# Attention with a bias on one core: the order of the first-pass loads and the place of the last two V copies

## The chip, the core and the metric

The kernel runs on one core of a Trainium2 chip. The metric is the device time of one execution in microseconds. A core has five engines that each work through a program of their own, in order: PE (TensorE, matmuls; its weight loads are listed as PEld), ACT (ScalarE, here the exps), DVE (VectorE), POOL (GpSimd, here only loads) and SP (SyncE, here copies inside the core's memory and stores). They wait for each other by semaphores. Sixteen DMA engines move the data that the queues of POOL, SP and ACT hand them.

## The reference

```python
head_dim = q.shape[-1]                      # q, k, v: (4, 8, 1024, 64), bias: (1, 1, 1024, 1024), float32
scale = 1.0 / np.sqrt(head_dim)
scores = scale * np.matmul(q, k.transpose(0, 1, 3, 2))
scores = scores + bias
scores_max = np.max(scores, axis=-1, keepdims=True)
attn = np.exp(scores - scores_max) / (np.sum(np.exp(scores - scores_max), axis=-1, keepdims=True) + 1e-8)
return np.matmul(attn, v).astype(np.float32)
```

There are 32 heads, and all of them share one bias of 1024 by 1024.

## The kernel before

**Slots.** The 32 heads are 16 pairs, and the 1024 queries of a head are 8 chunks of 128. One chunk of one head is a slot: a tile of 1024 keys by 128 queries of transposed scores. There are 256 slots. PSUM holds three such tiles, the places 0, 1 and 2 (`places`), and slots go to them in turn.

**The bias stays in the place.** A place works through the heads with one chunk. The bias of the chunk is put in once, by eight matmuls with the identity, at a start slot; for the next head PE adds the new head's K times Q and takes the old head's away, in one set of eight matmuls whose 128 contraction rows are 64 of the new head (`ko`, `qo`) and 64 of the old one with its sign turned (`ke`, `qe`). So a fill is 8 matmuls, at a start slot 16. A slot's fill has to wait until the slot before it in the same place has been read.

**Passes.** The first seven pairs go through chunks 0, 1 and 2 (slots 0 to 41), then 3 and 4 (slots 42 to 69, with start slots 42, 43 and 44, which need bias chunks 3 and 4), then 5, 6 and 7 (start slots 70, 71 and 72). The other nine pairs follow from slot 112 on: pair 14 begins at slot 154, pair 15 at slot 160.

**Exp and AV.** ACT reads a place and writes the exp as bf16 (`E`, a ring of 13). For 20 of the 256 slots DVE does it in six steps instead (`d_steps`: `dy`, `df`, `dt`, `df`, `dt`, `de`); only the first, `dy`, reads the place, so it is the one that lets the next fill in. These are called D slots; slots 38, 47, 50 and 150 are among them. Then PE multiplies the exp with V (AV, 8 matmuls into `po`). `vall` has a column of ones beside each head's V, which gives the sum. DVE divides (`rs`, `ob`; an evacuation of up to seven slots) and SP stores.

**Operands.** K and Q arrive as float32, are cast to bf16 by the loading DMA, are transposed by PE (`px`) and copied out by DVE (`ko`, `qo`) and, for the old head's half, by DVE or by an SP copy (`ke`, `qe`). Q of pairs 0 and 1 is loaded in two parts: the first three chunks at the beginning, the other five later as the rest (`qrest0`, `qrest1`), which is needed from slot 42 on. V is loaded into a ring of two tiles (`vland`) and copied by DVE into `vall` (line 492), so V of a pair is loaded no earlier than the copy of V of the pair two before.

**Loads.** All loads after the first few go through POOL's queue, in order. Those of the first pass are issued one after the other (`early`), as the list near the end of the kernel has them; each stands only for its buffer and its semaphore. From K of pair 7 on, `issue` puts a one-element copy to `tick` ahead of a load (line 467): it reads the load that lies two back in `flight`, so POOL issues nothing more until that has landed, and two loads at most are in flight.

**The order of the instructions** is made when the program is built. A planner walks through time with prices written by hand for each step and with estimated landing times of the loads (`raw_at` for K and Q, `vland_at` for V, `bias_at`). At each point it gives PE, ACT, DVE or SP the next step that is due by this reckoning. What it reckons sets the order only: on the chip each engine takes its steps in that order and waits where one is not ready. DVE's steps lie in `dve_q` with the time from which each may run and a priority; `move_v` enters the copy of V with the estimated landing. Which slots of place 2 become D slots is decided in `pe_cands`, in the kernel before by `backlog`, DVE's outstanding work.

Of the kernel before, what the change touches and what calls it, by code (L numbers as in the profile page):

```python
# [16 lines left out]
def kernel(  # L17
# [13 lines left out]
    nc = tc.nc  # L31
    B, H, S, D = q.shape
    P = 128
    NCH = S // P
# [13 lines left out]
    SPLIT, EARLY = 2, 7  # L48
# [3 lines left out]
    C0 = 3  # L52
# [17 lines left out]
    tick = consts.tile([1, 1], BF)  # L70
# [18 lines left out]
    slots = []  # L89
# [20 lines left out]
    NS = len(slots)  # L110
# [10 lines left out]
        at_place[x[0]] = s  # L121

    dslots = set()
    may_d = [x[0] == 2 and 36 < s < NS - 18 and not any(y[3] for y in slots[s:s + 4]) for s, x in enumerate(slots)]

    raws, lands, arrs = {}, {}, {}

# [18 lines left out]
    def load_q(pr, cs):  # L148
        if pr >= EARLY and 0 in BESIDE:
            return beside(pr, 0)  # L150

        t = consts.tile([P, 2, NCH - C0, D], BF, name=f"qrest{pr}") if cs.start else land.tile([P, 2, NCH, D], BF, name="q16")
        lands[pr, 0, cs.start] = t
        to = t[:, :, :cs.stop - cs.start, :]
        nc.gpsimd.dma_start(out=to.rearrange("p t c d -> p t (c d)"),
                            in_=qf[pr][:, :, cs.start * D:cs.stop * D])
        return to[:1, 1, cs.stop - cs.start - 1, D - 1:]
# [177 lines left out]
    with tc.manual_schedule():  # L335
# [101 lines left out]
        sp_q, t_sp = [], T0  # L437
        AHEAD, SLACK = 60, 300
        DEP = 115
        ROOM = 5000  # L440
        MARGIN = 0
        WINDOW = 4

# [17 lines left out]

        def issue(at, cost, depth, load, pr, *a):

            nonlocal t_dma
            if 0 < depth <= len(flight):
                what, t = flight[-depth]
                nc.gpsimd.tensor_copy(tick[:], what)  # L467
                at = max(at, t + 100)
            at = pool(at, 750)
            t_dma = max(t_dma + cost, at + 2200 + cost)  # L470
            flight.append((load(pr, *a), t_dma + 200))
            return t_dma + 200
# [17 lines left out]
        def move_v(pr):  # L490
            def run(t2):
                nc.vector.tensor_copy(vall[:, 2 * pr % VR:2 * pr % VR + 2, :, :D], lands[pr, "v"][:])  # L492
                v_at[pr] = t2 + 480 + L_DVE
                next_v(v_at[pr])
            dve_q.append((vland_at[pr], 0.3, 480, run))


        def early(kind, pr):
            if kind == "k":
                raw_at[pr, 1, 0] = issue(0, 1600, 0, load_k, pr) + SLACK  # L500
            elif kind == "q":
                cs = slice(0 if pr >= SPLIT else C0, NCH)
                raw_at[pr, 0, cs.start] = issue(0, 1600 if pr >= SPLIT else 1100, 0, load_q, pr, cs) + SLACK
            elif kind == "v":
                vland_at[pr] = issue(0, 1600, 0, load_v, pr)
                move_v(pr)
            else:
                bias_at[pr] = issue(0, 1600, 0, load_b, pr)

        def doubles(pr, which, c0, n, t2, urgent):  # L510
            if not which and pr >= EARLY:
# [63 lines left out]
        def pe_cands():  # L575

            out = []
            for x in range(3):
                if not queue[x] or queue[x][0] > next_fill + WINDOW:
                    continue  # L580
                s = queue[x][0]
                r = fill_ready(s)
                if r is not None and (before[s] is None or before[s] in used):
                    cost = FILL + BIAS * bool(slots[s][3] and s > 1)

                    def do(t, s=s, x=x, cost=cost):
                        nonlocal next_fill
                        fill(s)
                        filled[s] = t + cost + L_PE
                        queue[x].pop(0)  # L590
                        next_fill = min([y[0] for y in queue.values() if y], default=NS)
                        if may_d[s] and backlog(t) < ROOM and len(open_d) < 3:
                            dslots.add(s)
                            avq.remove(s)
                            start_d(s)
                        else:
                            acts.append(s)
                    out.append((max(t_pe, r), cost, do, 0, s))
# [92 lines left out]

        chains, d_wait, open_d = [], [], set()

        def backlog(t):
            x = max(0, t_dve - t) + sum(y[2] for y in dve_q if y[0] < t + 3000 and y[1] < 3)
            return x + sum(sum(y[0] for y in c) for c in chains) / 2 + sum(sum(y[0] for y in c[1:]) for r, s, c in d_wait) / 2

        def start_d(s):
            steps = d_steps(s)
            open_d.add(s)  # L700
# [68 lines left out]
        move_v(0)  # L769
        for x in ("k3", "q3", "v1", "k4", "q4", "v2", "k5", "q5", "v3", "k6", "q6", "v4", "v5", "b3", "q0", "q1", "b4", "v6", "b5", "b6", "b7"):  # L770
            early(x[0], int(x[1]))
        while next_fill < NS or next_act < len(acts) or avq or dav or dve_q or sp_q:
            c = []
            if next_act < len(acts):

                s = min(x for x in acts[next_act:] if filled[x] <= max(t_act, filled[acts[next_act]]))
                acts.remove(s)
                acts.insert(next_act, s)
                if next_act < NE or acts[next_act - NE] in av_done:
                    r = max(t_act, filled[s], av_done[acts[next_act - NE]] if next_act >= NE else 0)  # L780
# [62 lines left out]
```

## Time and profile before

| | |
|---|---|
| time, median of 3 runs (lowest to highest) | 233.25 us (232.87 to 233.69) |
| the profiled execution: its own time, its span | 235.16 us, 233.4 us |
| PE busy | 222.3 us (95%) |
| ACT busy | 221.1 us (95%), 237 exps of it 218.0 |
| DVE busy | 201.5 us (86%) |
| POOL busy | 63.4 us (27%) |
| DMA, HBM read and written | 29.36 MB and 8.39 MB |
| granted clock of PE | 0.997 |

The profile is of one execution and its times count from the beginning of the span. In a timeline each row has the start, the length, the engine, the line of the kernel, the operation with the tiles it writes and reads, the number of instructions put together in the row, and in brackets how long the engine had been idle just before and what ended that. "Busy" of a DMA in POOL's queue is the issue alone; its landing is given apart. The time of a run and the span of the profiled execution are not the same thing: a difference in the span is carried over to the median.

### The profile page before, as it was taken

How to read it: one execution, taken by the hardware profiler on the slowest of the kernel's cores; microseconds unless marked ns; L12 is line 12 of the kernel's file. 1: busy time of each engine (PE TensorE's matmuls, PEld its weight loads, DVE VectorE, ACT ScalarE, POOL GpSimd, SP SyncE). 2: the span in 40 equal slices, each digit the busy share in tenths (PEclk: the TensorE clock that was granted, in tenths of full speed). 3: DMA queues.
4: the chain of work that ended last, by engine and by line, in shares of the span. 5: the costliest groups of instructions: out<-in, count | busy, mean ns of one | idle time of the engine just before them, and what ended most of it. 6: DMA issues, size and time to landing. Idle time of an engine off the chain costs nothing. (4 is left out here: it accounts for less than half of the span.)

```text
span 233.4 us, 10703 instructions
## 1 busy us (share of the span) xinstructions
PE 222.3 (95%) x4671; PEld 209.3 (90%) x4671; DVE 201.5 (86%) x296; ACT 221.1 (95%) x241; POOL 63.4 (27%) x99
## 2 busy tenths in 40 slices
PE   7989999899999999999999997999999999999992
PEld 2869999798999999999999997999999999999982
DVE  2576677599999998999999869999998999999972
ACT  3799999988999999999999998999999999999993
POOL 8943135055446555245352310000000000000000
PEclk9999999999999999999999999999999999999998
DMA  6999979959999899999999992111111111221212
GB/s 206 206 205 215 224 166 158 229 121 150 120 191 137 131 159 183 204 196 157 197 163 201 204 194 68 44 42 39 44 37 42 45 42 42 65 59 42 66 48 56
DMA packets 55646, 29.75 MB, mean 127 GB/s; under 512 B 31472, under 2 KB 51952, under 8 KB 55600
## 3 DMA queue, kind: packets, MB, share of 16 engines
q0 software_dynamic: 30336, 14.06, 48.7%
q1 hardware_dynamic: 24832, 14.40, 22.6%
q8 instruction: 36, 0.59, 1.1%
q10 hardware_dynamic: 432, 0.62, 0.8%
q14 instruction: 10, 0.08, 0.1%
HBM read 29.36 MB, written 8.39 MB: 162 GB/s over the span
## 5 line engine op out<-in xcount | busy, mean ns | idle before, releaser
L258 ACT ACTIVATE E<-pl 128x1024 bf16<-128x1024 f32 (+1 forms) x237 | 218.0, 1089 | 4.3 <-PE pl L244 3.9
L312 PE MATMUL po<-vall,E 128*128 128x65 bf16 x1888 | 93.6, 194 | 0.9 <-ACT E L258 0.9
L312 PEld LDWEIGHTS <-E 128*128 128x128 bf16 x1888 | 78.1, 98 | 1.9 <-ACT E L258 1.2
L244 PE MATMUL pl<-qo,ko 128*128 128x128 bf16 x1024 | 77.3, 219 | 1.7 <-DVE dy L275 1.1
L244 PEld LDWEIGHTS <-ko 128*128 128x128 bf16 x1160 | 69.2, 98 | 4.5 <-issue 1.5
L244 PE MATMUL pl<-qe,ke 128*128 128x128 bf16 x888 | 66.8, 219 | 1.9 <-DVE qe L212 0.5
L244 PEld LDWEIGHTS <-ke 128*128 128x128 bf16 x888 | 53.2, 98 | 5.0 <-issue 1.3
L275 DVE TENSOR_SCALAR dy<-pl 128x1024 int32<-128x1024 f32 x20 | 24.4, 1220 | 2.1 <-PE pl L244 1.4
L322 DVE TENSOR_TENSOR ob<-po,rs 128x448 f32<-128x448 f32 (+2 forms) x39 | 23.2, 594 | 1.9 <-DVE rs L320 0.5
L295 DVE SCALAR_TENSOR_TENSOR de<-dy,dt 128x1024 uint16<-128x1024 int32 x20 | 24.4, 1218 | 0.0
L290 DVE SCALAR_TENSOR_TENSOR dt<-df,dt 128x1024 f32<-128x1024 f32 x20 | 24.4, 1218 | 0.0
L284 DVE SCALAR_TENSOR_TENSOR dt<-df 128x1024 f32<-128x1024 f32 x20 | 24.3, 1217 | 0.0
L287 DVE SCALAR_TENSOR_TENSOR df<-dt,df 128x1024 f32<-128x1024 f32 x20 | 24.3, 1216 | 0.0
L199 DVE COPY ko<-px 128x1024 bf16<-128x1024 bf16 (+1 forms) x16 | 10.7, 671 | 6.9 <-PE px L191 6.3
L165 POOL DMA_DIRECT2D v<-in_v_dram x16 | 11.4, 712 | 18.3 <-DVE vall L492 16.0
L138 POOL DMA_DIRECT2D q<-in_q_dram x18 | 16.0, 890 | 1.3 <-DMA out_dram<-ob 0.5
L201 DVE TENSOR_SCALAR qo<-px,sgn 128x1024 bf16<-128x1024 bf16 (+2 forms) x18 | 12.4, 688 | 4.4 <-PE px L191 3.6
L280 DVE TENSOR_SCALAR df<-dy 128x1024 f32<-128x1024 uint16 x20 | 13.8, 690 | 0.0
L241 PE MATMUL pl<-ident,braw 128*128 128x128 bf16 x136 | 11.5, 228 | 0.1
L145 POOL DMA_DIRECT2D k<-in_k_dram x15 | 11.0, 734 | 2.2 <-PE pl L244 1.0
L320 DVE RECIPROCAL rs<-po 128x7 f32<-128x7 f32 (+3 forms) x40 | 7.8, 195 | 4.4 <-PE po L312 4.0
L467 POOL COPY tick<-q 1x1 bf16<-1x1 bf16 x9 | 3.8, 421 | 24.7 <-DMA q<-in_q_dram 24.7
(54 smaller groups left out, 129.5 us busy)
## 6 DMA issues: line engine op xcount, KB each, us to landing
v<-in_v_dram POOLq DMA_DIRECT2D x16, 256.0 KB, 6.1
k<-in_k_dram POOLq DMA_DIRECT2D x15, 256.0 KB, 5.6
out_dram<-ob SPq DMA_DIRECT2D x32, 96.0 KB, 3.6
out_dram<-ob SPq DMA_DIRECT2D x45, 64.0 KB, 3.2
ke<-ko SPq DMA_DIRECT2D x22, 128.0 KB, 4.9
q<-in_q_dram POOLq DMA_DIRECT2D x18, 128.0 KB, 4.8
qe<-q SPq DMA_DIRECT2D x17, 128.0 KB, 4.9
out_dram<-ob SPq DMA_DIRECT2D x67, 32.0 KB, 1.8
```

Source lines behind the costliest of these rows:

```text
L138: nc.gpsimd.dma_start(out=t[:, :, y, :], in_=(qf, kf)[x][pr][:, y].rearrange("p (c d) -> p c d", d=D))
L201: nc.vector.tensor_scalar(t["qo"][:, cs, :], px[:], sgn[:], None, op0=ALU.mult)
L244: nc.tensor.matmul(to, kk[:, kc, :], qq[:, c, :], start=False, stop=True, skip_group_check=True)
L258: nc.scalar.activation(e[:, i:i + n].rearrange("p b x -> p (b x)"), places[slots[s][0]][:, i:i + n].rearrange("p b x -> p (b x)"), ACTF.Ex ...
L275: w.tensor_scalar(t["y"][:], places[slots[s][0]].rearrange("p b x -> p (b x)"), scale * LOG2E * 65536.0, 127.0 * 65536.0, op0=ALU.mult, op ...
L280: w.tensor_scalar(t["f"][:], t["lo"], G / 65536.0, None, op0=ALU.mult)
L284: w.scalar_tensor_tensor(t["t"][:], t["f"][:], -G, t["f"][:], op0=ALU.add, op1=ALU.mult)
L287: w.scalar_tensor_tensor(t["f"][:], t["t"][:], Q, t["f"][:], op0=ALU.mult, op1=ALU.add)
L290: w.scalar_tensor_tensor(t["t"][:], t["f"][:], V, t["t"][:], op0=ALU.add, op1=ALU.mult)
L295: w.scalar_tensor_tensor(etile[s].bitcast(U16).rearrange("p c q -> p (c q)"), t["y"][:], 1.0 / 512.0, t["t"][:], op0=ALU.mult, op1=ALU.add)
L312: nc.tensor.matmul(po[:, j + i, :], etile[s][:, kc, :], vall[:, slots[s][2] % VR, kc, :], start=j + i + kc == 0, stop=kc == NCH - 1, skip_ ...
L322: nc.vector.tensor_tensor(ob[:, :n, :], po[:, :n, :D], rs[:, :n, :].to_broadcast([P, n, D]), op=ALU.mult)
```

## The change

The early loads are taken out of the planning function `early`, which now only reckons, and are issued in a second loop in another order: the rests of Q of pairs 0 and 1 come ahead of V of pair 5 (before, they came behind V of pair 5 and bias chunk 3). The loads behind them, bias chunks 3 and 4, V of pair 6 and bias chunks 5 to 7, each get a copy to `tick` that reads the load two back, as the later loads have it. The planner's landing times of these loads stay as they were. Its entries in `flight` now carry other times, so that it reckons the loads from K of pair 7 on with landings 1.6 us later. The copies of V of pairs 14 and 15 may be placed 2.5 us later than before. The D slots are a list, `PLAN`, in place of the rule; it holds the same 20 slots that the rule chose.

```diff
@@ -121,9 +121,8 @@
     dslots = set()
-    may_d = [x[0] == 2 and 36 < s < NS - 18 and not any(y[3] for y in slots[s:s + 4]) for s, x in enumerate(slots)]
+    PLAN = (38, 47, 50, 59, 75, 78, 96, 108, 117, 129, 150, 159, 171, 177, 189, 195, 207, 216, 225, 234)
...
@@ -461,14 +459,17 @@
         def issue(at, cost, depth, load, pr, *a):
-            nonlocal t_dma
             if 0 < depth <= len(flight):
                 what, t = flight[-depth]
                 nc.gpsimd.tensor_copy(tick[:], what)
                 at = max(at, t + 100)
-            at = pool(at, 750)
-            t_dma = max(t_dma + cost, at + 2200 + cost)
-            flight.append((load(pr, *a), t_dma + 200))
+            t = lands_at(at, cost)
+            flight.append((load(pr, *a), t))
+            return t
+
+        def lands_at(at, cost):
+            nonlocal t_dma
+            t_dma = max(t_dma + cost, pool(at, 750) + 2200 + cost)
             return t_dma + 200
@@ -492,20 +493,24 @@
-            dve_q.append((vland_at[pr], 0.3, 480, run))
+            dve_q.append((vland_at[pr] + 2500 * (pr >= 14), 0.3, 480, run))
         def early(kind, pr):
             if kind == "k":
-                raw_at[pr, 1, 0] = issue(0, 1600, 0, load_k, pr) + SLACK
+                raw_at[pr, 1, 0] = lands_at(0, 1600) + SLACK
...
+        def early_load(kind, pr):
+            if kind == "q":
+                return load_q(pr, slice(0 if pr >= SPLIT else C0, NCH))
+            return {"k": load_k, "v": load_v, "b": load_b}[kind](pr)
@@ -589,7 +594,7 @@
-                        if may_d[s] and backlog(t) < ROOM and len(open_d) < 3:
+                        if s in PLAN:
@@ -769,6 +770,12 @@
         for x in ("k3", "q3", "v1", "k4", "q4", "v2", "k5", "q5", "v3", "k6", "q6", "v4", "v5", "b3", "q0", "q1", "b4", "v6", "b5", "b6", "b7"):
             early(x[0], int(x[1]))
+
+        for x in ("k3", "q3", "v1", "k4", "q4", "v2", "k5", "q5", "v3", "k6", "q6", "v4", "q0", "q1", "v5"):
+            flight.append((early_load(x[0], int(x[1])), t_dma))
+        for x in ("b3", "b4", "v6", "b5", "b6", "b7"):
+            nc.gpsimd.tensor_copy(tick[:], flight[-2][0])
+            flight.append((early_load(x[0], int(x[1])), t_dma + 200))
```

In the program that this builds, PE, DVE and ACT have the same instructions as before. PE's and DVE's order is the same for the first 82 us of the profile before; from there on K and Q pieces, V copies and D steps of pairs 7 to 15 stand some steps earlier or later. ACT's queue ends with one more store.

More of the change, by code (lines that the diff above doesn't have):

```diff
@@ L439 @@
         DEP = 115
-        ROOM = 5000
         MARGIN = 0
@@ L494, in run @@
                 next_v(v_at[pr])
-            dve_q.append((vland_at[pr], 0.3, 480, run))
+            dve_q.append((vland_at[pr] + 2500 * (pr >= 14), 0.3, 480, run))
         def early(kind, pr):
             if kind == "k":
-                raw_at[pr, 1, 0] = issue(0, 1600, 0, load_k, pr) + SLACK
+                raw_at[pr, 1, 0] = lands_at(0, 1600) + SLACK
             elif kind == "q":
-                cs = slice(0 if pr >= SPLIT else C0, NCH)
-                raw_at[pr, 0, cs.start] = issue(0, 1600 if pr >= SPLIT else 1100, 0, load_q, pr, cs) + SLACK
+                raw_at[pr, 0, 0 if pr >= SPLIT else C0] = lands_at(0, 1600 if pr >= SPLIT else 1100) + SLACK
             elif kind == "v":
-                vland_at[pr] = issue(0, 1600, 0, load_v, pr)
+                vland_at[pr] = lands_at(0, 1600)
                 move_v(pr)
             else:
-                bias_at[pr] = issue(0, 1600, 0, load_b, pr)
+                bias_at[pr] = lands_at(0, 1600)
+        def early_load(kind, pr):
+            if kind == "q":
+                return load_q(pr, slice(0 if pr >= SPLIT else C0, NCH))
+            return {"k": load_k, "v": load_v, "b": load_b}[kind](pr)
         def doubles(pr, which, c0, n, t2, urgent):
@@ L692 @@
         chains, d_wait, open_d = [], [], set()
-        def backlog(t):
-            x = max(0, t_dve - t) + sum(y[2] for y in dve_q if y[0] < t + 3000 and y[1] < 3)
-            return x + sum(sum(y[0] for y in c) for c in chains) / 2 + sum(sum(y[0] for y in c[1:]) for r, s, c in d_wait) / 2
         def start_d(s):
```

## The prediction

> **What bounds the kernel now.** I read the page first: one line of busy time, one row of the DMA engines in 40 slices of 5.8 us.
>
> ```profile
> PE 222.3 (95%) x4671; PEld 209.3 (90%) x4671; DVE 201.5 (86%) x296; ACT 221.1 (95%) x241; POOL 63.4 (27%) x99
> ...
> DMA  6999979959999899999999992111111111221212
> ```
>
> ACT and PE are both at 95%, DVE at 86%. Loads keep the DMA engines at nine tenths up to slice 24, with two dips in the first pass: slice 5 (29.2 to 35.0 us) and slice 8 (46.7 to 52.5). Next, ACT's timeline, to see where the busiest engine stands still (first column start, then length; in brackets the idle time just before).
>
> ```profile
> 17.19 30.08 ACT L258 ACTIVATE E<-pl 128x1024 bf16<-128x1024 f32 x32 [0.21 <-PE pl L244]
> 47.53 1.02 ACT L258 ACTIVATE E<-pl 128x1024 bf16<-128x1024 f32 x1 [0.26 <-PE pl L244]
> 48.76 1.02 ACT L258 ACTIVATE E<-pl 128x1024 bf16<-128x1024 f32 x1 [0.21 <-PE pl L244]
> 50.00 4.69 ACT L258 ACTIVATE E<-pl 128x1024 bf16<-128x1024 f32 x5 [0.21 <-PE pl L244]
> 55.28 17.52 ACT L258 ACTIVATE E<-pl 128x1024 bf16<-128x1024 f32 x19 [0.59 <-PE pl L244]
> ...
> 143.24 86.31 ACT L258 ACTIVATE E<-pl 128x1024 bf16<-128x1024 f32 x94 [0.87 <-PE pl L244]
> ```
>
> Unhindered, exps start 0.904 us apart (start times in the trace). Where ACT stood, the next slots are 42 to 44 (0.26, 0.21, 0.21), slot 51 (0.59) and slot 153 (0.87), always for a fill of PE. So I looked at what held PE and DVE there: PE at 42, DVE up to 53, and PE at 54.
>
> ```profile
> 42.11 0.47 PE L191 MATMUL px<-ident,qrest 128*64 128x128 bf16 x10 [0.78 <-DMA qrest<-in_q_dram]
> ```
>
> ```profile
> 42.62 0.55 DVE L201 TENSOR_SCALAR qo<-px,sgn 128x640 bf16<-128x640 bf16 x1 [1.88 <-PE px L191]
> ...
> 46.96 0.43 DVE L492 COPY vall<-v 128x1024 bf16<-128x1024 bf16 x1 [0.85 <-DMA v<-in_v_dram]
> ...
> 52.86 1.22 DVE L275 TENSOR_SCALAR dy<-pl 128x1024 int32<-128x1024 f32 x1
> ```
>
> ```profile
> 53.35 0.42 PE L312 MATMUL po<-vall,E 128*128 128x65 bf16 x8
> 54.13 0.61 PE L244 MATMUL pl<-qe,ke 128*128 128x128 bf16 x8 [0.36 <-DVE dy L275]
> 54.57 0.61 PE L244 MATMUL pl<-qo,ko 128*128 128x128 bf16 x8
> ```
>
> PE ended its AV at 41.33 and stood 0.78 for the rest of q of pair 0. DVE stood 1.88 behind that, then 0.85 for V of pair 6 (landed 46.9), and from 46.96 worked without a gap until the `dy` of slot 47 was done at 54.08; the fill of slot 50 waited for that one, and slot 51's exp behind it. The third place, DVE and then PE:
>
> ```profile
> 133.61 0.43 DVE L492 COPY vall<-v 128x1024 bf16<-128x1024 bf16 x1 [0.40 <-DMA v<-in_v_dram]
> ...
> 138.33 0.43 DVE L492 COPY vall<-v 128x1024 bf16<-128x1024 bf16 x1 [1.86 <-DMA v<-in_v_dram]
> ...
> 141.32 1.22 DVE L275 TENSOR_SCALAR dy<-pl 128x1024 int32<-128x1024 f32 x1
> ```
>
> ```profile
> 142.59 0.61 PE L244 MATMUL pl<-qo,ko 128*128 128x128 bf16 x8 [1.14 <-DVE dy L275]
> ```
>
> DVE stood 0.40 for V of pair 13 and 1.86 for V of pair 14; `dy` of slot 150 came at 141.32 though its fill had ended at 139.84, PE waited 1.14 for the place, and exp 153 started 1.94 after its predecessor: 1.94 - 0.904 = 1.03 lost. Last, POOL's timeline for the loads of the first pass:
>
> ```profile
> 27.20 0.70 POOL L165 DMA_DIRECT2D v<-in_v_dram  x1 [4.39 <-DVE vall L492]
> 32.77 0.74 POOL L165 DMA_DIRECT2D v<-in_v_dram  x1 [4.88 <-DVE vall L492]
> ...
> 34.05 1.42 POOL L155 DMA_DIRECT2D qrest<-in_q_dram  x2
> ...
> 36.02 0.70 POOL L165 DMA_DIRECT2D v<-in_v_dram  x1
> ```
>
> The V at 32.77 is pair 5's. It stood 4.88 for the copy of V of pair 3, with eight loads queued behind it in order; the DMA engines were at 0.37 from 32 to 34 us.
>
> **The change, part by part.**
>
> *The rests go first.* POOL is free from 27.90. With the rests ahead of V5 they issue at 27.9 and 28.6, not 34.05 and 34.75. V5 is not moved: its wait ends at 32.5 either way. The rests queue behind V4, which landed at 32.9; they had landed 1.3 apart (42.0 and 43.3), so they land at about 34.2 and 35.5 (call the second T). Bounds of T: 34.3, if they slip in beside V4, and 37.8, if the first takes the 3.6 us that lay between bias chunk 3 (38.4) and it. V5 came 4.0 after its issue and was copied at 36.89; behind the rests it lands by about 37, and DVE's idle 0.89 before its next step (38.19) covers that; beyond 0.9 it would cost what it exceeds.
>
> PE's transposes of the rest then start at 41.33. Everything behind moves up 0.78, except where ACT has not freed the place: slot 39's fill (43.67) needs slot 36's exp (42.09, took 1.04, unmoved) to end at 43.13, so from there the gain is 0.54. The bias fills of slots 42 to 44 are 1.23 apart on PE and stay so: exp 44 moves from 50.00 to 49.46.
>
> *Loads from bias chunk 3 on wait for all but the last two.* POOL gets six one-element copies to `tick` (0.18 to 1.09 each, means 0.42 to 0.86 by tile; I take 0.5): 3 us on an engine busy 27%, which by itself costs nothing. What counts is who is queued behind. Chunk 3 waits for the second rest, chunk 4 for V5, V6 for chunk 3, chunks 5 to 7 for chunk 4, V6 and chunk 5. Issue to landing with little in flight was 4.0 (V5), 4.9 (chunk 3), 3.9 (K7); I take 4.4. Chunk 3 lands at T + 0.5 + 4.4 = 40.4, needed at 45.8; chunk 4 at about 42, needed at 47.0; V6 at L = T + 2 x (0.5 + 4.4) = 45.3, not 46.9. Bounds of L: 34.3 + 2 x (0.2 + 3.9) = 42.5, and 37.8 + 2 x (1.1 + 4.9) = 49.8. Chunks 5 to 7 land at about 46.5, 50 and 51 and are used from slot 70 on (exp at 71.6); K7 and Q7 go out near 50 and 51, as before.
>
> If each of the two ticks waited behind a whole long DVE step (1.22), L would be 46.7 and the gain below 0.2 (rival 1). I stay with 0.5, since DVE's steps from 35 to 41 are 0.2 to 0.75 long. The Trainium skill (SBUF — State Buffer, section SBUF: two separate sides) gives the reason for such a wait: VectorE and GpSimd lock each other out of a shared port pair for a whole instruction; the trace's 1.09 against 0.18 for one element fits.
>
> *DVE in the first pass.* With the rest early DVE reaches V6's copy at 46.11 - 0.78 = 45.33. `dy` of slot 47 was the end of the gapless run, so it moves by 46.96 minus the larger of 45.33 and L, but no earlier than its fill, which ends at 52.02 - 0.54 = 51.48: 51.6, not 52.86, if V6 lands by 45.6. Then slot 50's place is free at 52.83 and its fill no longer waits for DVE; it follows AV 36 (53.35 - 0.54 + 0.26 = 53.07), slot 51's fill 0.44 later, its exp 0.71 after that: 54.22, not 55.28. **Gain A = 1.06**, or 46.9 - L where that is less: 0 if V6 lands when it did, and a loss if later. From 45.3 I take 1.06; by the bounds of L, A is 1.06 down to -2.9.
>
> *The last two copies of V.* In the order built, V14's copy stands behind `dy` of slot 150, and V15's behind that, one evacuation and one `df` step; K15's copy-out goes ahead of V13's copy. From V13's copy to `dy` of 150 were 141.32 - 133.61 = 7.71; less the stall 1.86, V14's copy 0.35, V15's 0.33 and K15's copy-out 0.69: 4.48. V13's load waits for the copy of V11, which moves behind one more 1.13 step, about what A brings forward; so V13 lands at 133.6 again and DVE could do `dy` at 138.1, while its fill ends at 139.84 - 1.06 = 138.8. The fill ends last, with 0.7 to spare, and PE's wait of 1.14 goes. V14's load waits for V12's copy (130.19; with one step more in front and A off, about 130.8), goes out at 131.8 and lands after 5.0 to 7.2 (V12's and V14's own), by 139.0; its copy is due after `dy`, at 140.0. V15: out at 134.6, plus 6.2, 140.8; due at 141.9. **Gain B = 1.03.** Bounds: 0, if the wait moves to another step, and 1.86, all of DVE's stall.
>
> *The planner's order from 83 us on.* D slots are the same 20 (now a list), and so are the number and kind of steps on PE and DVE; the K and Q pieces and V copies of pairs 7 to 15 shift by a few steps because later loads are planned 1.6 us later. Nothing in the trace prices an order that did not run. Beyond 0.904 per exp, ACT lost 1.1 in 72 to 141 us and 0.7 after 145; a new order can win or lose about half of each, so 0 with +-0.9 for the range. One more store goes through ACT's queue at the end: 0.38, done by 230.44, while the last store waited for DVE until 230.53: nothing; at most 0.4.
>
> **Sum.** The profiled execution took 235.16, its span 233.4 plus 1.8 around it; the median is 233.25. 235.16 - 1.06 - 1.03 = 233.07; the same 2.09 off the median gives **231.2**.
>
> **The rivals.**
> 1. *V6 comes no earlier.* Three waits in a row (rest, chunk 3, V6) eat the gain: L of 46.9 or later, DVE stands as before, A is 0. For it: the upper bounds of T; against: L of 45.3 has 1.6 to spare. 233.25 - 1.03 = 232.2.
> 2. *The V stall only moves.* V13's wait of 0.40 grows, or V14 is still out when its copy is due; `dy` of 150 is late again. For it: V12 landed at 129.9 and was copied at 130.19, so these loads live on small margins. Only A: 232.2.
> 3. *Slower: two in flight is too few.* If each load took 7.2 (V14's), L would be 35.5 + 2 x (0.5 + 7.2) = 50.9, A = -4.0, and with B the time 236.2. It decides from L = 47.9 (even); from 48.6 it is slower by 0.7. For it: chunks 4 to 7 took 9.5 to 12.6; against: those lay behind a long queue, which the waits forbid. The Trainium skill (DMA: Bandwidth & Descriptors, section Anatomy of one DMA — SWDGE (gpsimd) path) speaks against such waits: most of a load's fixed 2 us is completion, paid again at every wait. By its formula 256 KB take an estimated 2.6, L is 41.7 and A is still whole; the trace's 3.9 to 4.9 is dearer.
> 4. *It does not do what it says.* ACT was to stand at the bias fills of slots 70 to 72 anyway (0.34 at 73.14) and elsewhere for PE, and what is won is given back there: 233.2. Against: after these two places ACT runs 75 and 94 exps in unbroken rows.
>
> **How the numbers follow.** Chances: forecast 0.60, rival 1 0.15, rival 2 0.11, rival 4 0.05, slower 0.09. A measurement of this kernel tells about 0.3% (0.7 us) from no change, so the first three are faster: 0.86; same 0.05; slower 0.09. Range: the forecast less half of the order's 0.9 and a little of B's upper bound gives 230.5; upwards it takes in rivals 1 and 2 with half a microsecond on top, 232.7. That leaves out rivals 3 and 4 and a few tails, 2 in 10.
>
> **What would show it.** Right: no wait of PE or DVE for the rest of q near 42; V6's copy near 45.4 with an idle of at most 0.3 before it; slot 51's exp near 54.2; no idle of ACT near 141; V14's copy behind `dy` of 150. Wrong: DVE waiting for V6 beyond 46, or for V13 to V15 by over 1 us, or new idle times of ACT after 83 us that add up to over 1 us.

## The result and the profile after

The changed kernel took 234.55 us in the median of 22 runs (233.01 to 236.59), and the kernel before, on the same chip, 233.25 us in 22 runs (232.67 to 236.32). The ratio of the mean times, without the one slow run on each side, is 1.0047, with a 95% interval of 1.0025 to 1.0070: slower by about 1.1 us, where 2.05 us less were predicted. The profiled execution took 234.76 us, its span 233.0 (before: 235.16 and 233.4). So the profiled executions stand in the opposite order of the medians. The 235.16 that the prediction started from lies above all but one of those 22 runs of the kernel before.

Of the page of the changed kernel, the busy times and the rows of ACT and the DMA engines in 40 slices of 5.8 us:

```profile
PE 221.6 (95%) x4671; PEld 209.0 (90%) x4671; DVE 201.5 (86%) x296; ACT 221.0 (95%) x241; POOL 66.3 (28%) x105
...
ACT  3799999988999999999999999999999999999993
...
DMA  6999999686999999999999993111111111221212
```

The engines' sums are as before, but for POOL's six added copies. In the DMA row slice 5 (counted from 0, as in the prediction), which held a dip before, is full: the rests of q now lie in it. The dips are now slices 7 to 9 (40.8 to 58.2 us).

POOL's timeline of the changed kernel, from the rests of q on:

```profile
28.16 1.42 POOL L154 DMA_DIRECT2D qrest<-in_q_dram  x2
33.05 0.75 POOL L164 DMA_DIRECT2D v<-in_v_dram  x1 [3.47 <-DVE vall L493]
35.24 0.18 POOL L777 COPY tick<-qrest 1x1 bf16<-1x1 bf16 x1 [1.44 <-DMA qrest<-in_q_dram]
35.47 0.54 POOL L159 DMA_DIRECT2D braw<-in_bias_dram  x1
37.52 0.37 POOL L777 COPY tick<-v 1x1 bf16<-1x1 bf16 x1 [1.51 <-DMA v<-in_v_dram]
37.98 0.54 POOL L159 DMA_DIRECT2D braw<-in_bias_dram  x1
42.17 0.18 POOL L777 COPY tick<-braw 1x1 bf16<-1x1 bf16 x1 [3.64 <-DMA braw<-in_bias_dram]
42.72 0.70 POOL L164 DMA_DIRECT2D v<-in_v_dram  x1 [0.37 <-DVE qo L200]
...
53.03 0.70 POOL L144 DMA_DIRECT2D k<-in_k_dram  x1
...
55.70 1.34 POOL L137 DMA_DIRECT2D q<-in_q_dram  x1 [0.29 <-issue]
```

The second rest landed at 35.2 (predicted: 35.5) and PE did not wait for it. But bias chunk 3, issued at 35.47, took 6.6 us to land (42.1), so V of pair 6 went out at 42.72, landed 4.2 us later, at 46.9, and K of pair 7 was issued at 53.03. DVE's timeline at both places shows what this did:

```profile
46.91 0.43 DVE L493 COPY vall<-v 128x1024 bf16<-128x1024 bf16 x1 [1.18 <-DMA v<-in_v_dram]
...
52.82 1.22 DVE L274 TENSOR_SCALAR dy<-pl 128x1024 int32<-128x1024 f32 x1
...
135.50 0.43 DVE L493 COPY vall<-v 128x1024 bf16<-128x1024 bf16 x1 [1.06 <-DMA v<-in_v_dram]
...
140.29 1.23 DVE L274 TENSOR_SCALAR dy<-pl 128x1024 int32<-128x1024 f32 x1 [0.22 <-PE pl L243]
141.43 0.42 DVE L493 COPY vall<-v 128x1024 bf16<-128x1024 bf16 x1
```

The copy of V of pair 6 (46.91) stood 1.18 us, and `dy` of slot 47 came at 52.82, as in the profile before (52.86; there the first exp starts at 7.98, here at 8.20). The copy of V of pair 14 (141.43) stands behind `dy` of slot 150 and waits for nothing, as predicted; but V of pair 13, which had cost DVE 0.40, now cost it 1.06. Slot 50's fill in PE's timeline, and ACT's timeline at the two places:

```profile
54.09 0.61 PE L243 MATMUL pl<-qe,ke 128*128 128x128 bf16 x8 [0.54 <-DVE dy L274]
```

```profile
49.79 4.69 ACT L257 ACTIVATE E<-pl 128x1024 bf16<-128x1024 f32 x5 [0.21 <-PE pl L243]
55.24 17.52 ACT L257 ACTIVATE E<-pl 128x1024 bf16<-128x1024 f32 x19 [0.77 <-PE pl L243]
...
127.72 9.34 ACT L257 ACTIVATE E<-pl 128x1024 bf16<-128x1024 f32 x10
137.21 33.38 ACT L257 ACTIVATE E<-pl 128x1024 bf16<-128x1024 f32 x36 [0.16 <-PE po L311]
```

Slot 51's exp started at 55.24 (55.28 before, 54.22 predicted), behind an idle of 0.77. The last row shows only 0.16, but the exp before it had started 1.36 us earlier (two starts in the trace), which is 0.46 more than the unhindered 0.904.

### The profile page after: what moved, and what is told of

Its sections match the earlier page's. It is cut to its first block, busy times and chain, and to the rows that moved or that the text cites. A ratio compares the mean times of both kernels' runs of the same rounds, so it can differ in the third digit from the quotient of the medians.

```text
span 233.0 us, 10673 instructions
## 1 busy us (share of the span) xinstructions
PE 221.6 (95%) x4671; PEld 209.0 (90%) x4671; DVE 201.5 (86%) x296; ACT 221.0 (95%) x241; POOL 66.3 (28%) x105
## 5 line engine op out<-in xcount | busy, mean ns | idle before, releaser
L240 PEld LDWEIGHTS <-braw 128*128 128x128 bf16 x136 | 9.9, 149 | 0.2 <-issue 0.2
```

What stands on the lines that cost most here:

```text
L240: nc.tensor.matmul(to, braw[:, c, :].rearrange("p (kp kc) -> p kc kp", kc=NCH)[:, kc, :], ident8[:], start=i == 0, stop=False, skip_group_ ...
```

## What the experiments vary

The theory after this result was: the six waits leave too few bytes in flight, so everything from bias chunk 3 on lands later; DVE then stands at copies of V, and what is behind them on DVE (`dy`, evacuations) holds PE and ACT. Its rivals were the order of the rests, the moved order of steps from 82 us on, and that the profiled executions mislead. The variants have the changed kernel's second loop in this form:

```python
        TICKS = ("b3", "b4", "v6", "b5", "b6", "b7")
        for x in (
            ...
            "v4", "q0", "q1", "v5", "b3", "b4", "v6", "b5", "b6", "b7"):
            if x in TICKS:
                nc.gpsimd.tensor_copy(tick[:], flight[-2][0])
            flight.append((early_load(x[0], int(x[1])), t_dma + 200))
```

The last line holds the times that make the planner reckon the later loads 1.6 us later (the "shift"). Where a variant is without it, that line is `at = bias_at[int(x[1])] if x[0] == "b" else t_dma` and `flight.append((early_load(x[0], int(x[1])), at))`, which gives back the times of before. "Late" means the copies of V that the planner places later. Ratios are against the kernel before on the same chip (29 to 35 runs of it), each variant with 12 runs (6 of e8_ticks, 13 of e12_again). The own time is that of one profiled execution, and "DVE for V" is the time that DVE stood at copies of V in it.

| run | rests first | waits | shift | late | ratio and interval | own time | K7 issued | DVE for V |
|---|---|---|---|---|---|---|---|---|
| e1_null | no | no | no | no | 1.0015 [0.9990, 1.0040] | 233.43 | 49.47 | 1.7 |
| e2_waits | yes | two | no | no | 1.0079 [1.0042, 1.0115] | 236.56 | 52.38 | 7.1 |
| e3_vlate | no | no | no | 14, 15 | 1.0010 [0.9981, 1.0039] | 233.32 | 49.71 | 1.2 |
| e4_rests | yes | no | no | no | 1.0056 [1.0025, 1.0087] | 235.00 | 48.12 | 0.6 |
| e4b_rests | yes | no | no | no | 1.0024 [0.9997, 1.0052] | 233.89 | 47.87 | 0.6 |
| e8_ticks | no | two | no | no | 1.0150 [1.0112, 1.0187] | 237.94 | 55.16 | 5.8 |
| e7_shift | no | no | yes | no | 1.0007 [0.9989, 1.0025] | 233.74 | 49.50 | 0.6 |
| e5_no_shift | yes | two | no | 14, 15 | 1.0022 [0.9999, 1.0045] | 234.16 | 51.57 | 2.5 |
| e12_again (the changed kernel) | yes | two | yes | 14, 15 | 1.0041 [1.0021, 1.0062] | 239.32 | 53.45 | 9.1 |
| e9_v6late | yes | two | yes | 6, 14, 15 | 1.0026 [1.0004, 1.0048] | 234.21 | 52.29 | 2.2 |
| e10_depth3 | yes | three | yes | 14, 15 | 1.0024 [0.9997, 1.0050] | 233.47 | 49.10 | 0.8 |
| e13_nowaits | yes | no | yes | 14, 15 | 1.0022 [0.9993, 1.0051] | 234.57 | 47.16 | 1.9 |
| e11_vall | no | no | no | 6 to 15 | 1.0007 [0.9993, 1.0022] | 233.75 | 49.74 | 0.0 |
| e14_waits_vall | yes | two | no | 6 to 15 | 1.0005 [0.9988, 1.0023] | 234.02 | 52.74 | 1.4 |
| e15_depth3_vall | yes | three | no | 6 to 15 | 1.0007 [0.9985, 1.0029] | 233.88 | 49.19 | 0.4 |

## The parts of the change, one by one

**The program of before, with the list of D slots** (e1_null): no part of the change but `PLAN`. Against the changed kernel:

```diff
-            dve_q.append((vland_at[pr] + 2500 * (pr >= 14), 0.3, 480, run))
+            dve_q.append((vland_at[pr], 0.3, 480, run))
...
-        TICKS = ("b3", "b4", "v6", "b5", "b6", "b7")
+        TICKS = ()
...
-            "v4", "q0", "q1", "v5", "b3", "b4", "v6", "b5", "b6", "b7"):
+            "v4", "v5", "b3", "q0", "q1", "b4", "v6", "b5", "b6", "b7"):
...
-            flight.append((early_load(x[0], int(x[1])), t_dma + 200))
+            at = bias_at[int(x[1])] if x[0] == "b" else t_dma
+            flight.append((early_load(x[0], int(x[1])), at))
```

> The kernel before with the list of D slots in place of the rule: the same program, so the time of before, 233.25, and a second profile of it. Theory 1 (the profiled execution of before, 235.16, was a poor one, 1.9 over the median, and its two stalls are not in a usual execution): a profile with its own time near 233.3 and a span near 231.5, in which DVE's waits for V of pair 6 and pair 14 add up to well under 1 us and exp 51 starts before 54.8. Theory 2 (the stalls are always there, the loss of the changed kernel comes from what it adds): the same stalls, 0.85 for V of pair 6 and near 1.9 for V of pair 14, whatever the execution's time.

Ratio 1.0015 [0.9990, 1.0040], as no change has to give. Its profile is the more telling part: a second execution of the program of before, PE's and DVE's order being the same step by step in the two traces. It took 233.43 us; the median of the kernel before on that chip is 233.39, that of e1_null's own 12 runs 234.01. DVE's timeline at the two copies on which the prediction's gains rested, and ACT's:

```profile
46.02 0.43 DVE L493 COPY vall<-v 128x1024 bf16<-128x1024 bf16 x1 [0.39 <-DMA v<-in_v_dram]
...
136.12 0.43 DVE L493 COPY vall<-v 128x1024 bf16<-128x1024 bf16 x1 [0.19 <-DMA v<-in_v_dram]
```

```profile
49.74 22.28 ACT L257 ACTIVATE E<-pl 128x1024 bf16<-128x1024 f32 x24 [0.20 <-PE pl L243]
...
127.67 43.30 ACT L257 ACTIVATE E<-pl 128x1024 bf16<-128x1024 f32 x47
```

V of pair 6 cost DVE 0.39 and V of pair 14 0.19, not 0.85 and 1.86, and ACT runs 24 exps unbroken over slot 51 and 47 over slot 153. The two stalls that the prediction meant to take away (1.06 and 1.03) weren't there. They belonged to the execution profiled before, which was 1.91 over its median. Counted from the first exp (7.98 there, 8.22 here), that execution is 1.01 behind this one at slot 51, 1.95 at slot 153 and 1.97 at the last, so the two stalls are nearly the whole difference between the two. The profiles of e3_vlate, e7_shift and e11_vall, which have the loads of before too, don't show them either: the exps of slots 49 and 51 start 1.13 apart in each (1.65 in the profile before), those of 152 and 153 0.90 to 0.92 (1.94). Against e1_null's execution the changed one is 0.74 us behind by slot 73's exp (74.97 against 74.22 in the traces; it is the "exp 70" of e9_v6late's expectation, which counts ACT's exps) and 1.16 behind by slot 161's (149.12 against 147.96).

**The copies of V of pairs 14 and 15 alone** (e3_vlate): e1_null with the first line of its diff put back.

```diff
-            dve_q.append((vland_at[pr], 0.3, 480, run))
+            dve_q.append((vland_at[pr] + 2500 * (pr >= 14), 0.3, 480, run))
```

> Only the 2.5 us for the copies of V of pairs 14 and 15 are changed; the loads are those of before. If the later order is the cost, about 234.5, with waits of PE for evacuations or for V near 135 and after. If it does what the prediction's step B says, 232.2 against an execution that had the stall, and no gain (233.2) if a usual execution does not have it (theory 1).

Ratio 1.0010 [0.9981, 1.0039], and a profile like e1_null's: own time 233.32, DVE for V 1.2. Where DVE hardly stands, there is nothing to gain that can be measured, and the copies' place costs nothing measurable either.

**The planner's shift alone** (e7_shift): e1_null with the changed kernel's last line of the loop.

```diff
-            at = bias_at[int(x[1])] if x[0] == "b" else t_dma
-            flight.append((early_load(x[0], int(x[1])), at))
+            flight.append((early_load(x[0], int(x[1])), t_dma + 200))
```

> The loads and their waits as before, and the planner's reckoning of the loads from K of pair 7 on later by 1.6 us as in the changed kernel, so that only the order of the steps past 82 us differs. Theory one (the order of steps costs nothing by itself): ratio 0.998 to 1.002. Theory two (the moved order is what costs): ratio 1.003 to 1.006, with idle time of ACT past 82 us of over 0.7 us in all.

Ratio 1.0007 [0.9989, 1.0025]: with the loads of before, the moved order past 82 us costs nothing that can be measured.

**The rests and the waits, in the order of before** (e2_waits): the changed kernel's loads, and every other engine's order that of before.

```diff
-            dve_q.append((vland_at[pr] + 2500 * (pr >= 14), 0.3, 480, run))
+            dve_q.append((vland_at[pr], 0.3, 480, run))
...
-            flight.append((early_load(x[0], int(x[1])), t_dma + 200))
+            at = bias_at[int(x[1])] if x[0] == "b" else t_dma
+            flight.append((early_load(x[0], int(x[1])), at))
```

> Only the loads of the first pass are changed, rests first and the six waits; the orders of PE, DVE, ACT and SP are those of before. If the waits are the cost (bias chunk 3 and V of pair 6 one after the other at 4 to 6.6 each), V of pair 6 lands at 46 to 47 or later and the kernel is slower than before by 0.5 to 1.5: 233.8 to 234.8. If the later order is the cost, this one is within 0.3% of before or faster: 232.5 to 233.9.

Ratio 1.0079 [1.0042, 1.0115], the largest loss with the rests first and more than the 0.5 to 1.5 us expected. Its list of DVE's waits (engine, line, what it waited for; total, times, longest) and its ACT timeline past 80 us:

```profile
DVE vall L493 <- DMA v<-in_v_dram: 7.1, 8, 1.4
```

```profile
85.86 4.77 ACT L257 ACTIVATE E<-pl 128x1024 bf16<-128x1024 f32 x5 [0.50 <-PE pl L243]
...
132.50 5.61 ACT L257 ACTIVATE E<-pl 128x1024 bf16<-128x1024 f32 x6 [0.46 <-PE po L311]
138.70 5.65 ACT L257 ACTIVATE E<-pl 128x1024 bf16<-128x1024 f32 x6 [0.59 <-PE pl L243]
```

K of pair 7 went out at 52.38, not 49.47, and the chain behind it stayed late: eight copies of V had to be waited for, 7.1 us in all (5.6 of it at six copies behind K of pair 7), where e1_null had four with 1.7. The idle times of ACT appear 30 us and more after the last of the added waits. But this execution took 236.56 us, 1.15 over the median of e2_waits (235.41), whose 12 runs go from 233.54 to 237.02: the 7.1 us are those of one of its slower executions.

**The rests first alone** (e4_rests, and the same program once more, e4b_rests): e2_waits without its waits.

```diff
-        TICKS = ("b3", "b4", "v6", "b5", "b6", "b7")
+        TICKS = ()
```

> Only the rests of q go ahead of V of pair 5, no waits added; all other orders are those of before. The prediction's step A without the waits: transposes of the rest without a wait near 41.4, V of pair 6 at about 45.5 or earlier as its load follows V of pair 4's copy at 35; 232.2 if the stall is there in a usual execution. Theory 1: 233.2. If moving the rests ahead is itself the cost (V of pair 5 late, copies and stores crowded from 28 to 35), 234 or more and a wait of DVE for V of pair 5 over 0.9.

> The same program as e4_rests (the rests of q ahead of V of pair 5, no added waits, every engine's order as before), to see whether its 1.0056 and the two losses of its profile come again: a start about 1.0 us later, and a pause of PE of 1.28 us at 42.2 in the transposes of the rests. Theory one (the rests' order costs by itself, because more of the traffic then lies in 28 to 42 us and something small that PE needs comes late behind it): ratio 1.004 to 1.007 and the pause at about 42 is there again, over 0.8 us. Theory two (the order is harmless and the profile was of an unlucky execution): ratio 0.999 to 1.003, no pause over 0.3 us there.

Ratios 1.0056 [1.0025, 1.0087] and 1.0024 [0.9997, 1.0052]: by the first a loss, by the second perhaps none. The loads are not late here (K of pair 7 at 48.12 and 47.87, DVE for V 0.6 each time). PE's timeline of e4_rests at the transposes of the first rest:

```profile
42.24 0.25 PE L190 MATMUL px<-ident,qrest 128*64 128x128 bf16 x2
43.52 0.41 PE L190 MATMUL px<-ident,qrest 128*64 128x128 bf16 x8 [1.04 <-issue]
```

PE paused 1.04 us after the second of ten transposes and waited for no semaphore. In e4b_rests the pause is at the same instruction, but 0.26 long. The start that was a microsecond late in e4_rests (exp 0 at 9.18 instead of 8.2) was not there in e4b_rests (8.33).

**The waits alone, in the old order of loads** (e8_ticks): e1_null with the six waits.

```diff
-        TICKS = ()
+        TICKS = ("b3", "b4", "v6", "b5", "b6", "b7")
```

> The load order of before, and the six added waits alone; every engine's order as before. Theory one (the waits cost, because bias chunk 3 and what is behind it is issued later, the whole chain of loads from K of pair 7 on, at 49.5 to 50.4 before, moves to 52 or later, and V copies are waited for): ratio 1.004 to 1.010, K of pair 7 issued past 51.5, DVE waits for V of pairs 7 to 14 of together over 3 us. Theory two (it is the order of the rests that costs): ratio 0.998 to 1.002 and the first slots past 42 as before.

Ratio 1.0150 [1.0112, 1.0187], 3.5 us: more than either theory gave. In this order the second load behind V of pair 5 is the first rest, so bias chunk 4 waits for it, and V of pair 6 was issued at 43.62. The list of waits from 40 to 58 us:

```profile
ACT E L257 <- PE pl L243: 3.2, 4, 2.6
...
DVE vall L493 <- DMA v<-in_v_dram: 2.8, 1, 2.8
...
PE pl L243 <- DVE dy L274: 2.0, 1, 2.0
```

Here the chain of the prediction stands in the open: DVE 2.8 at V of pair 6, PE 2.0 for the `dy` behind it, ACT 2.6 in one piece at the fill. In this order limiting the loads in flight is what costs, and the rests' earlier place gives about half of it back (1.0079 in e2_waits).

## What in the waits costs

**Without the shift** (e5_no_shift): the changed kernel with before's times in `flight`.

```diff
-            flight.append((early_load(x[0], int(x[1])), t_dma + 200))
+            at = bias_at[int(x[1])] if x[0] == "b" else t_dma
+            flight.append((early_load(x[0], int(x[1])), at))
```

> The changed kernel without the planner's 1.6 us: the rests first, the six waits, the last two V copies later, and the other steps in the order of before. Theory one (the waits delay the later loads, and the later placing by the planner gives part of it back): slower than the changed kernel, ratio 1.006 to 1.009, with the DVE waits of e2_waits for V of pairs 7 to 13, 5 us or more together, and without that for V of pair 14. Theory two (the moved order is what costs): faster than the changed kernel, ratio 1.000 to 1.003.

Ratio 1.0022 [0.9999, 1.0045]. I had expected it slower than the changed kernel; if anything it is faster, and DVE stood 2.5 us for V, not 5. So nothing shows that the shift gives anything back under the waits. From e2_waits it differs by the later copies of pairs 14 and 15 alone, and its ratio is about half a per cent lower, but the two intervals overlap. That these two copies are worth so much isn't shown: PE and DVE do the same steps in the same order until DVE comes to the copy of pair 14 (139.71 in e2_waits), yet by slot 140's exp, counted from the first, the profile of e2_waits is already 1.56 us behind this one. So most of the difference between 7.1 and 2.5 us lies between two executions, not two orders.

**The changed kernel once more** (e12_again): no edit.

> The changed kernel once more, with runs on the same chip as the other three, and a second profile of it. If its loss is from the mechanism read in its first profile, ratio 1.003 to 1.007, V of pair 6 lands at 46.5 to 47.2, K of pair 7 is issued at 52 to 54 and DVE stands at V of pair 13 again by about 1. If the first profile was of an unusual execution, these differ by over 1 us.

Ratio 1.0041 [1.0021, 1.0062], as the first time (1.0047). Its profiled execution took 239.32 us, 4.35 over the median of 234.97, so whether the first profile is a usual one isn't settled by it.

**V of pair 6 copied later** (e9_v6late): the changed kernel, and DVE does the second `qe` and the evacuation before that copy.

```diff
-            dve_q.append((vland_at[pr] + 2500 * (pr >= 14), 0.3, 480, run))
+            dve_q.append((vland_at[pr] + 2500 * (pr >= 14) + 2600 * (pr == 6), 0.3, 480, run))
```

> The changed kernel, but the copy of V of pair 6 is placed 2.6 us later by the planner: it then stands behind the second qe and the evacuation that it held up in the changed kernel's profile (idle 1.18 us before the copy at 46.91); apart from that only the copy of V of pair 13 changes its place, by one step. Theory one (DVE held by V of pair 6 is what shifts the slots past 55 by 0.77 us): no idle of DVE over 0.3 us at 45 to 48, slot times at exp 70 as in the null run (74.2 against 75.0), ratio to before 1.000 to 1.003. Rival (the loss lies in the later loads and the moved order past 82 us): ratio still 1.004 to 1.006.

DVE no longer stood at that copy, and slot 73's exp came at 74.04 where the changed kernel has 74.97 and e1_null 74.22. The first exps start at 7.96, 8.20 and 8.22, so counted from there it is 0.7 us ahead of the changed kernel and level with e1_null (0.08 behind): the first 0.7 us of the loss in the profile were this copy. The rest stayed: V of pair 13 cost DVE 1.7 in this profile. Ratio 1.0026 [1.0004, 1.0048].

**Three loads in flight** (e10_depth3):

```diff
-                nc.gpsimd.tensor_copy(tick[:], flight[-2][0])
+                nc.gpsimd.tensor_copy(tick[:], flight[-3][0])
```

> The changed kernel, but the six added waits read the load three back, so that three loads are in flight and not two. Theory one (two in flight move too few bytes, 0.71 of the DMA engines' time in 40 to 46 us against 1.18 before, and that is why bias chunk 4, V of pair 6 and K of pair 7 come late): V of pair 6 lands before 46.3, K of pair 7 is issued at 51.5 or earlier instead of 53.0, ratio 1.000 to 1.003. Rival (DMA engines share their time anyway, so the depth changes nothing): K of pair 7 at 52.5 to 53.5, ratio 1.004 to 1.006.

POOL's timeline of this run, V of pair 6 and K of pair 7:

```profile
38.29 0.71 POOL L164 DMA_DIRECT2D v<-in_v_dram  x1 [0.18 <-DVE vall L493]
...
44.33 0.18 POOL L777 COPY tick<-v 1x1 bf16<-1x1 bf16 x1 [0.28 <-DMA v<-in_v_dram]
...
49.10 0.71 POOL L144 DMA_DIRECT2D k<-in_k_dram  x1
```

V of pair 6 went out 4.4 us earlier than in the changed kernel and had landed when the `tick` at 44.33 read it, and K of pair 7 was issued 3.9 us earlier, even before e1_null's. The table of stretches shows why, row 40 to 46 us (busy PE, PEld, DVE, ACT, POOL, the granted clock, the DMA engines' busy share, which can exceed 1 in this view, GB/s), first of the kernel before, then of the changed one, then of this one:

```profile
40.00:46.00 6.00, 5.22 (x114) 4.81 (x112) 3.89 (x8) 5.77 (x7) 0.00 (x0) 1.00 1.18 231
```

```profile
40.00:46.00 6.00, 5.79 (x128) 5.32 (x125) 4.42 (x9) 6.00 (x7) 1.61 (x4) 1.00 0.71 130
```

```profile
40.00:46.00 6.00, 5.93 (x128) 5.39 (x126) 4.47 (x10) 6.00 (x7) 2.33 (x6) 1.00 1.04 179
```

Two in flight moved 130 GB/s, three 179, an unlimited queue 231 (and 227 in e13_nowaits below, which has the changed kernel's order of loads and no waits). So the depth is what made the loads late. DVE's one wait for V in this profile is the 0.84 for V of pair 5 at 37.64, ahead of steps with time to spare; the span is 231.7, e1_null's. The ratio, 1.0024 [0.9997, 1.0050], says that about half of the loss is gone, by its middle; its interval reaches from no loss to the whole of it.

**The changed kernel without the waits** (e13_nowaits):

```diff
-        TICKS = ("b3", "b4", "v6", "b5", "b6", "b7")
+        TICKS = ()
```

> The changed kernel without the six added waits; the rests first and every engine's order as in the changed kernel. Theory one (the waits are the cause: two in flight move too few bytes): K of pair 7 issued at 48 to 49.5 as in e4_rests and e4b_rests, DVE waits for V of together under 1.5 us, ratio 0.999 to 1.002. Rival (the rests' order and the moved order are the cause): ratio 1.003 to 1.006, as the changed kernel.

Ratio 1.0022 [0.9993, 1.0051], between the two forecasts and not told apart from the changed kernel's. No wait for V of pair 6, and K of pair 7 at 47.16; but DVE stood 1.64 for V of pair 13, and PE paused 0.53 in the transposes of the first rest. So V of pair 13 needs no late loads to be late: among the profiles with the changed kernel's order past 82 us, e12_again's left aside, the wait is in three of four (1.06, 1.67 in e9_v6late, 1.64 here, none in e10_depth3). That V is loaded into the tile that the copy of V of pair 11 frees, which comes at 127.81 here and at 126.65 in e1_null, and the load goes out at 128.77 instead of 127.60. It isn't that alone: in e10_depth3 the load goes out as late (128.57), but lands 4.4 us later, here 6.5.

**All copies of V from pair 6 on placed later**: with the loads of before (e11_vall), with the changed kernel's loads and waits (e14_waits_vall), and with waits three deep (e15_depth3_vall). All three have e1_null's last line of the loop and the same order on every engine but POOL; the first also has e1_null's loads, the third `flight[-3]`.

```diff
-            dve_q.append((vland_at[pr] + 2500 * (pr >= 14), 0.3, 480, run))
+            dve_q.append((vland_at[pr] + 2000 * (pr >= 6), 0.3, 480, run))
```

> The loads and waits of before, and the copies of V of pairs 6 to 15 placed 2.0 us later each, so that DVE seldom stands at such a copy. Theory one (DVE standing at V copies, 1.7 us in 4 waits in the null run and 4.5 in the profiled execution of before, shifts the slots in the slower executions of before): a median 0.3 to 0.8 us below before, ratio 0.996 to 0.999, and together under 0.6 us of DVE waits for V. Rival (these waits are absorbed by the work behind them, and the moved order gives something else late): ratio 0.999 to 1.004.

> The loads and the six waits of the changed kernel, with the engines' order of e11_vall, in which the copies of V of pairs 6 to 15 come 2.0 us later by the planner. Theory one (the late loads act only through DVE standing at V copies): DVE waits for V of together under 1.5 us, ratio 0.999 to 1.002, as e11_vall's 1.0007. Rival (they act in another way too, through K and Q of the later pairs or through PE): ratio 1.003 to 1.006.

> As e14_waits_vall, but the six waits read the load three back, as in e10_depth3. Theory one: V of pair 6 lands at 44 to 45, K of pair 7 is issued near 49, DVE waits for V under 0.5 us, ratio 0.997 to 1.001, the fastest of the variants with the rests first. Rival (the rests first cost by themselves): ratio 1.002 to 1.005.

1.0007 [0.9993, 1.0022], 1.0005 [0.9988, 1.0023] and 1.0007 [0.9985, 1.0029]. The second shows how late loads act. It is e2_waits with one line edited (and the order that the planner makes of it, which by itself, in e11_vall, costs nothing measurable), has the changed kernel's loads and waits and K of pair 7 nearly as late (52.74), and costs nothing that can be measured. DVE's waits for V in it and, for comparison, in the changed kernel:

```profile
DVE vall L493 <- DMA v<-in_v_dram: 1.4, 2, 0.9
```

```profile
DVE vall L493 <- DMA v<-in_v_dram: 2.8, 3, 1.2
```

So the late loads cost through the place of V's copies in DVE's order, and in no other way that shows. The hoped-for gain of e11_vall over before did not come, though DVE stood at no copy of V at all, and no variant beats the kernel before.

## Why the prediction was wrong

- **"The same 2.09 off the median".** This step failed first, and it takes the whole forecast gain away. Steps A and B priced stalls of one execution that took 1.91 us more than the median, and for that execution the prices were about right: 1.06, and 2.09 with B, against the 1.01 and 1.95 by which it is behind e1_null (above). e1_null, the same program, has neither (0.39 at V of pair 6 and 0.19 at V of pair 14, no idle of ACT at slots 51 and 153), and e11_vall, in which DVE waits for no V, is no faster than before (1.0007). What could be won off the median was nothing that can be measured, not 2.09. The loss comes from the steps below.
- **The rests go first.** Right as to times: issued at 28.16 and 28.9, the second landed at 35.2 (T = 35.5). It brought nothing: where PE had waited 0.78, in e1_null its weight load waited 0.17, and slot 49's exp starts at 53.38 there and at 53.42 in the changed kernel.
- **Step A, "I take 4.4".** This term was too small. Issue to landing was 4.2 and 4.3 for the two V but 6.6, 5.9, 5.0, 5.0 and 4.7 for the bias chunks, so L was 46.9 and not 45.3, inside the stated bounds and at the value that rival 1 names. On V6's way, T was 35.2 for 35.5, the issues followed the landings by 0.3 and 0.7 for twice 0.5, and chunk 3 took 6.6 for 4.4: that one load is the miss. Against e1_null (46.00) V of pair 6 even came later; e9_v6late puts its price at 0.7 us in the profile.
- **"K7 and Q7 go out near 50 and 51, as before".** Wrong by 3.0 and 4.7: 53.03 and 55.70. The prediction did follow the waits through chunks 6 and 7, which it had landing at about 50 and 51, but with the same 4.4 for each load; they landed at 52.5 and 55.1. Since K7 came out "as before", the sum has no term for later loads of the later pairs. In e2_waits, where no copy is placed later, they show: 5.6 us of DVE waits for V behind K7 in its profiled execution.
- **Step B.** Right in its mechanism: V of pair 14 is copied behind `dy` of slot 150, without idle. There was no stall of 1.03 to take away, and V of pair 13 became the wait, 1.06: rival 2.
- **The planner's order, 0 with +-0.9.** Right by itself (e7_shift, 1.0007). Together with the late copies of pairs 14 and 15 it makes V of pair 13 a wait in three profiles of four; what that costs the median was not settled.
- **Rival 3, "two in flight is too few".** Right in its mechanism, at 0.09 the least believed but rival 4, and wrong in its point of decision: it was reckoned from 46.9 for V of pair 6, the value of the first profile, and asked for L of 47.9. e1_null has 46.0, and L of 46.9 was enough. The objection, that the long landing times of bias chunks 4 to 7 came from the queue in front, holds for about half of their 9.5 to 12.6 us; what stays is 4.7 to 5.9. The Trainium skill (DMA: Bandwidth & Descriptors, section Anatomy of one DMA — SWDGE (gpsimd) path) puts most of a load's fixed cost of about 2 us into completion. The prediction held that against the waits, and the direction came out so, though no run here tells completion from the moving of the data. The 2.6 us that the prediction estimated for 256 KB from that section's formula is 0.4 to 0.6 of the 4.2 to 6.6 here.

What stays open: how the changed kernel's 0.47% divides between the waits and the moved order, since e13_nowaits, without the waits, lies between; and what the rests first cost by themselves. Without waits they cost 0.56%, 0.24% and 0.22% in three tries, of which only the first is clear of zero. Their three profiles show the pause of PE in the first rest's transposes: the third transpose starts 1.20, 0.42 and 0.69 later than in e1_null, counted from the second (idle times of PE: 1.04, 0.26 and 0.53). At slot 49, counted from the first exp, they stand 0.64, 0.21 and 0.41 behind e1_null. With the loads of before it is late in three profiles of five, by 0.39, 0.36 and 0.10; with three loads in flight by 0.10 and 0.21; with two in none.

The kept traces show what ends this pause. A DMA queue of the kind "instruction" makes 36 transfers of 16 KB in an execution, which fits PE's 9342 matmuls and weight loads, one for about 260. In all 17 profiles the third transpose starts 1.21 us or more after the end of the last such transfer before it; in the eight where it is late, 1.21 to 1.50 after that end. So PE most likely waited for its next instructions. The transfer itself began between 36.5 and 39.2 us with two loads in flight, at 39.3 and 39.5 with three, between 38.7 and 39.8 with the loads of before, and between 39.8 and 41.1 with the rests first and no waits; that the crowd of loads held it up is argued from this, not tested.

## What to carry to other kernels

Take a second profile, or at least set the one at hand against the median, before pricing a stall: one that stands only in an execution 2 us over the median is a part of the spread, and taking it away need not win anything in the median. A wait that keeps two loads in flight lowers what the DMA engines move (130 against 227 to 231 GB/s here, in 40 to 46 us), so follow the last load of the group through to who queues behind it, tens of microseconds on. Where a late load meets an engine with other work due, moving its consumer back in that engine's order can be worth more than moving the load forward: e14_waits_vall is e2_waits with that one edit, and its ratio fell from 1.0079 to 1.0005.

## What had not been expected of the hardware

Two executions of one program, 1.7 us apart, differ in the landing of loads (V of pair 6 at 46.0 and 46.9) while the busy times of PE, DVE and ACT agree within 0.6. And PE can pause up to 1.04 us between two matmuls of one step, here always before the same one, with no semaphore to wait for; each time it went on 1.21 to 1.50 us after a 16 KB transfer of an instruction queue had ended.
